# A bidirectional SSD mixer on one core: another order of a group's stages, with the state products placed between the parts of the next projection

## The chip, the cores and the metric

The kernel runs on one core of a Trainium2 chip. The metric is the device time of one execution in microseconds (us). Three runs of the kernel before took 1614.75, 1614.91 and 1621.10 us; their median is 1614.91.

## The reference

A trunk of two layers works on 512 tokens of 1024 features, batch 1, in float32. Layer 0 mixes tokens with a bidirectional Mamba-2 (SSD), layer 1 with a two-sided Hyena convolution; each is followed by a SwiGLU and a gated embedding. The change touches the SSD mixer alone:

```python
z, xbc, dt = split(h @ in_w)                    # 2048, 2048 + 2*8*128, 64 columns
xbc = silu(centred_depthwise_conv(xbc, 5 taps)) # x, B, C
for each direction, chunk of 128 tokens:        # 8 groups of 4 heads of 64
    acum = cumsum(dt * a)
    scores = (C @ B.T) * exp(acum_l - acum_s) * dt      # masked, per head
    y = scores @ x + (C @ state) * exp(acum)
    state = state * exp(acum_last) + B.T @ (exp(acum_last - acum) * dt * x)
y = (y_f + y_b + x * d_skip) * silu(z)
y = y / rms(y over a group's 256 features) * norm_w
out = y @ out_w
```

## The kernel before, in words

**Matmuls.** A float32 weight is split into a rounded part `w_hi` and a rest `w_lo`, an activation likewise, and a product is three matmuls (`mm3`, L291 to L293) per tile of 128x128 weights and 512 tokens. `dense` (L295) runs such products over a list of tiles. Matmuls of full float32 (transposes, state work) show twice in the trace for one in the code where they are not transposes.

**Weights.** All weights lie in DRAM in the order of use, in blocks of 8 tiles. `weight` (L277) emits a block (`emit_block`, L267) up to two blocks ahead: a transfer on SP's queue (L269), the cast to `w_hi` on ScalarE (L273), the difference `w_lo` on VectorE, or on GpSimd for every second block here (L274). There are three buffers each of raw, hi and lo. One group of the mixer takes six blocks: B, C, x0, x1 and two for z.

**The mixer.** `ssd` (L540) goes over 8 groups `g`. For one group:
- `mix_in` (L575) projects 128 features each of B, C, x0, x1. The evacuation is the convolution: one ScalarE operation (L581) and four on VectorE (L585), then tanh and one more operation (L587, L588).
- `mix_z` (L659) projects the gate.
- `mix_pre` (L674) transposes B (L678) and x (L685), forms CB, the product of C and B by chunk (L690), the weighted inputs `xw` (two operations of VectorE, L698), the state sums `contribution` (L709, four matmuls in `pS`) and the `carry` from chunk to chunk: copies on ScalarE (L718, L720), a product on GpSimd into the scratch tile `stt` (L714), a sum on VectorE (L715). The result is `ST`, the states at the chunks' entries. Last it starts `y` as x times `d_skip` on GpSimd (L730).
- `mix_exp` (L734) makes the decay matrices `M` of the four heads: a broadcast transfer into `FB` on SP's queue (L740, 512 KB, four buffers), two selects on GpSimd (L742), eight exponentials on ScalarE (L746), an add and a product on VectorE (L748, L749).
- `mix_rest` (L752) does the products within chunks (L759) and adds them to `y` (L761), then the state products for each of the four chunks (L765), scales them into `yo` (L768) and adds (L770), then gates (L773 to L775) and takes the sums of squares (L778) with a scratch tile that has the same two buffers as `stt`.
- `scales` and `finish` (L781, L787) normalise two groups at a time and transpose them for the output projection (L793, L322, L323).

PSUM has four buffers `mm` for projections and four `aux` for everything else.

**What sets the order.** The loop at L809 is staggered by one group: while group g is projected, group g - 1 is finished. But the program's order is only a priority. The framework in which the kernel is written lays out each engine's queue when the program is built: it keeps a model of the engines' times and gives each engine, whenever that model has it free, the instruction that stands earliest in the program among those that are ready, and it takes buffers in the same way. On the chip each queue then runs in that fixed order and waits where the chip is later than the model. So instructions of later stages are found between those of earlier ones; the time line of TensorE shows C's matmuls of the next group between two state products.

The loop's order before is this, for an iteration g:

```python
mix_in(g: C, x0, x1); mix_exp(g-1); mix_z(g); mix_in(g+1: B)
mix_rest(g-1); finish(g-3) if g is odd; mix_pre(g); finish(g-2) if g is odd
```

Of the kernel before, what the change touches and what calls it, by code (L numbers as in the profile page):

```python
# [35 lines left out]
def order_mk(name, ms, ks, hold=0):  # L36
    """(name, k, m) in the order of use; the first `hold` columns get their last k late."""
# [143 lines left out]
def constants():  # L181
# [7 lines left out]
    # token order: parity, block of 128, place  # L189
# [5 lines left out]
    # [q, p, (par, blk), 256]  # L195
    out["dec"] = np.ascontiguousarray(dec[perm].reshape(4, P, 4, 256).transpose(2, 1, 0, 3))
    # angular frequencies w and pi / 2 - w, for w = 2 pi (f + 1/2) / 1024, f < 128
    fr = (np.concatenate([np.arange(P), 255 - np.arange(P)]) + 0.5) * (2.0 * math.pi / 1024.0)
    n = np.arange(T)
    cs = np.stack([np.cos(np.outer(n, fr)), np.sin(np.outer(n, fr))])  # [cs, n, f]  # L200
    ch = cs[:, perm].reshape(2, 2, 2, P, 256)  # [cs, par, blk, p, f]
    out["CH"] = np.ascontiguousarray(ch.transpose(3, 1, 0, 2, 4).reshape(P, 2048).astype(f))
    perm = np.array([4 * m + r for r in range(4) for m in range(P)])
    cf = cs[:, perm, :P].reshape(2, 4, P, P)  # [cs, r, m, f]
    out["CF"] = np.ascontiguousarray(cf.transpose(2, 1, 0, 3).reshape(P, 1024).astype(f))
    ci = cs.reshape(2, P, 2, 2, 2, P) / 512.0  # [cs, m, b, par, fch, f], t = 4 m + 2 b + par
# [8 lines left out]
def body(ctx, tc, d, out_):  # L215
# [24 lines left out]
    # ---- constants and parameters  # L240
# [13 lines left out]
    # ---- weight stream  # L254
# [40 lines left out]
    def dense(keys, rhs, evac, at=0, then=None):  # L295
        """keys in order of use; rhs[k] = (hi, lo); evac(m, ps); then() after the first `at` keys"""
# [16 lines left out]
    # ---- norms: sum of squares over features, on every partition  # L313
    def split(src, hi=None, lo=None, scale=None):
        """src * scale as hi + lo"""
# [10 lines left out]
    class Norm:  # L326
# [15 lines left out]
        def finish(self, keep=True):  # L342
            """1 / rms per token as a column, then as a row on every partition"""
# [23 lines left out]
    # ---- Hyena filters in the frequency domain  # L367
# [16 lines left out]
    def forward_h(C, mv, U, pool):  # L384
        """As forward and butterfly, for the cosines of one series and the sines of another:
        even and odd places apart; mv(cs, par, blk) = (hi, lo), [128, 256]"""
# [18 lines left out]
    def forward(CF, mv):  # L405
        """Sums over m of 256 channels' places t = 4 m + r times cos (cs 0) and sin (cs 1) of w t, at 128 w:
        [cs, 0] and [cs, 1] with r = 0, 1 and 2, 3 for cos, r = 1, 0 and 3, 2 for sin.
        mv(cs, r) = (hi, lo), [128 m, 256]"""
# [106 lines left out]
    def after(ins, f, *args):  # L515
        if ins is None:
            return f(*args)
        with tc.issue_after(ins.ins):
            return f(*args)

    # ---- per-layer embedding projection
    def ple_in(pool, i, tags):
        pr = {}
        for k in range(2):
# [602 lines left out]
```

## Time and profile before

| | us |
|---|---|
| median of three runs | 1614.91 |
| span of the profiled execution, first to last instruction | 1613.2 |
| its own time beyond the span | not listed; the median is 1.7 more than the span |
| TensorE busy (matmul) | 1569.7 |
| VectorE, ScalarE, GpSimd busy | 1055.6, 675.9, 203.1 |
| mixer loop, z of group 1 to z of group 7 | 96 to 386 |
| granted TensorE clock, mean | 0.996 of full speed |

How to read it: times in views are us from the span's start, durations of single instructions in a table of lines are ns. PE is TensorE's matmuls, PEld its weight loads, DVE VectorE, ACT ScalarE, POOL GpSimd, SP the queue that issues transfers (SPq is its sequencer). `L765` is line 765 of the kernel. `out<-in` are tile names. In brackets, or behind the last bar, stands idle time before an instruction and what ended it. Matmuls overlap each other, so the pace is read from start to start, not from their durations.

### The profile page before, as it was taken

To read this page: it belongs to the slowest core of one execution; us is meant where nothing else is said; L and a number is where in the kernel's file an instruction comes from. 1 tells how busy PE (TensorE), PEld (TensorE's weight loads), DVE (VectorE), ACT (ScalarE), POOL (GpSimd) and SP (SyncE) were. 2 spreads that over 40 slices of the span, in tenths; PEclk is the share of its full clock that TensorE was granted. 3 is DMA by queue.
4 is the path that set the end of the run, shared out by engine and by line. 5 is a ranking of instruction groups with operands and counts; after the bars stand their busy time and mean duration, and the time that the engine had idled before them with its cause. 6 is when DMAs were issued, how large, how long until landed. Compare 5 with 4: busy or idle time off the path is not lost.

```text
span 1613.2 us, 19944 instructions
## 1 busy us (share of the span) xinstructions
PE 1569.7 (97%) x7746; PEld 1303.4 (81%) x7746; DVE 1055.6 (65%) x1447; ACT 675.9 (42%) x1111; POOL 203.1 (13%) x153
## 2 busy tenths in 40 slices
PE   8999999999999999999999999999999999999998
PEld 5888777878788788888888887788888888888887
DVE  6778987879855765464345578999874434434464
ACT  6575555756434332232233445333243223222355
POOL 1244433443100000000000001332000000000000
PEclk9999999999999999999999999999999999999999
DMA  6343324343133233342333345333122332322332
GB/s 241 113 151 109 114 78 122 113 120 116 53 134 118 79 131 118 104 137 92 98 98 94 103 148 172 105 104 100 58 92 92 93 103 92 104 93 93 122 98 79
DMA packets 56006, 176.80 MB, mean 110 GB/s; under 512 B 5959, under 2 KB 7175, under 8 KB 54760
## 3 DMA queue, kind: packets, MB, share of 16 engines
q1 hardware_dynamic: 46864, 151.17, 29.5%
q10 hardware_dynamic: 9048, 24.36, 4.2%
q8 instruction: 61, 1.00, 0.3%
q14 instruction: 33, 0.27, 0.1%
HBM read 164.89 MB, written 10.62 MB: 109 GB/s over the span
## 4 chain that ended last, share of the span: by engine, by line
PE 72%; DVE 16%; DMA 4%; ACT 4%; issue 2%; POOL 1%; SPq 0%; ACTq 0%; DVEq 0%; POOLq 0%
PE mm_ps L291 21%; PE mm_ps L293 21%; PE mm_ps L292 21%; DMA FB<-FRd 3%; DVE pre L585 2%; DVE w_lo L274 2%; DVE xw L698 1%; PE aux_ps L292 1%; PE aux_ps L291 1%; PE aux_ps L293 1%; DVE M L748 1%; ACT w_hi L273 1%; ACT FB L746 1%; DVE act L320 1%; POOL FB L742 1%
## 5 line engine op out<-in xcount | busy, mean ns | idle before, releaser
L291 PE MATMUL mm_ps<-act,w_hi 128*128 128x512 f32 (+1 forms) x1856 | 722.5, 390 | 0.0
L292 PE MATMUL mm_ps<-act,w_hi 128*128 128x512 f32 (+1 forms) x1856 | 720.9, 388 | 0.9 <-DVE act L320 0.9
L293 PE MATMUL mm_ps<-act,w_lo 128*128 128x512 f32 (+1 forms) x1856 | 719.4, 388 | 0.2 <-DVE w_lo L274 0.2
L273 ACT CAST w_hi<-w_raw 128x1024 fp32r<-128x1024 f32 x248 | 259.8, 1051 | 603.9 <-PE mm_ps L292 427.5
L291 PEld LDWEIGHTS mm_ps<-act,w_hi 128*128 128x128 f32 x1856 | 348.6, 188 | 74.7 <-issue 5.5
L292 PEld LDWEIGHTS mm_ps<-act,w_hi 128*128 128x128 f32 x1856 | 348.6, 188 | 73.9 <-issue 3.6
L293 PEld LDWEIGHTS mm_ps<-act,w_lo 128*128 128x128 f32 x1856 | 348.7, 188 | 72.0 <-issue 2.4
L274 DVE TENSOR_TENSOR w_lo<-w_raw,w_hi 128x1024 fp32r<-128x1024 f32 x213 | 265.8, 1249 | 131.9 <-ACT w_hi L273 131.8
L274 POOL TENSOR_TENSOR w_lo<-w_raw,w_hi 128x1024 fp32r<-128x1024 f32 x35 | 97.6, 2790 | 738.1 <-ACT w_hi L273 716.4
L857 DVE TENSOR_TENSOR fb<-mm_ps,R 128x512 f32<-128x512 f32 x44 | 30.4, 692 | 130.7 <-PE mm_ps L293 130.7
L585 DVE SCALAR_TENSOR_TENSOR pre<-mm_ps,par,pre 128x511 f32<-128x511 f32 (+1 forms) x128 | 93.1, 739 | 3.2 <-ACT pre L581 3.0
L746 ACT ACTIVATE FB<-FB,bcol 128x128 f32<-128x128 f32 x256 | 79.8, 392 | 23.0 <-POOL FB L742 22.8
L854 DVE TENSOR_TENSOR fa<-mm_ps,R 128x512 f32<-128x512 f32 x44 | 30.4, 691 | 89.4 <-PE mm_ps L293 89.4
L865 DVE TENSOR_TENSOR h<-h,mm_ps 128x512 f32<-128x512 f32 x48 | 33.0, 687 | 72.8 <-PE mm_ps L293 72.8
L668 PE MATMUL mm_ps<-w_lo,act 128*128 128x256 f32 x256 | 72.6, 284 | 0.0
L669 PE MATMUL mm_ps<-w_hi,act 128*128 128x256 f32 x256 | 72.4, 283 | 0.0
L667 PE MATMUL mm_ps<-w_hi,act 128*128 128x256 f32 x256 | 72.4, 283 | 0.0
L742 POOL TENSOR_SCALAR_AFFINE_SELECT FB<-FB 128x512 f32<-128x512 f32 x64 | 53.6, 861 | 68.1 <-DMA FB<-FRd 60.7
L668 PEld LDWEIGHTS mm_ps<-w_lo,act 128*128 128x128 f32 x256 | 49.1, 192 | 0.3
L667 PEld LDWEIGHTS mm_ps<-w_hi,act 128*128 128x128 f32 x256 | 49.1, 192 | 0.3
L669 PEld LDWEIGHTS mm_ps<-w_hi,act 128*128 128x128 f32 x256 | 49.1, 192 | 0.0
L319 ACT CAST act<-fb 128x512 fp32r<-128x512 f32 x44 | 27.4, 622 | 29.3 <-DVE fb L858 29.3
(261 smaller groups left out, 1633.8 us busy)
## 6 DMA issues: line engine op xcount, KB each, us to landing
w_raw<-W SPq DMA_DIRECT2D x248, 512.0 KB, 3.5
FB<-FRd SPq DMA_DIRECT2D x32, 512.0 KB, 5.4
pjd<-ppo ACTq DMA_DIRECT2D x16, 256.0 KB, 3.6
Hd<-Ht ACTq DMA_DIRECT2D x4, 1024.0 KB, 3.8
Ht<-Hd ACTq DMA_DIRECT2D x4, 1024.0 KB, 4.8
pj<-pjd ACTq DMA_DIRECT2D x12, 256.0 KB, 3.7
h<-xT SPq DMA_DIRECT2D x8, 256.0 KB, 5.7
dec<-dec ACTq DMA_DIRECT2D x4, 512.0 KB, 4.3
```

The costliest lines, as they stand in the source:

```text
L273: A.copy(hi, raw)
L274: (G if pool_lo(b) else V).tensor_sub(lo, raw, hi.bitcast(F32))
L291: PE.matmul(ps, whi, xhi, start=start, stop=False)
L292: PE.matmul(ps, whi, xlo, start=False, stop=False)
L293: PE.matmul(ps, wlo, xhi, start=False, stop=stop)
L585: V.scalar_tensor_tensor(pre[:, a:b], ps[:, a + o:b + o], pc("cw", 5 * c + j), pre[:, a:b], ALU.mult, ALU.add)
L667: PE.matmul(o, xhi[:, cs], whi, start=k == 0 and c % 2 == 0, stop=False)
L668: PE.matmul(o, xhi[:, cs], wlo, start=False, stop=False)
L669: PE.matmul(o, xlo[:, cs], whi, start=False, stop=k == KD - 1 and c % 2 == 1)
L742: G.affine_select(FB[:, dr], FB[:, dr], pattern=[[0, NC], [1 - 2 * dr, P]], compare_op=ALU.is_ge, fill=BIG, base=0, channel_multiplier=2 * ...
L746: A.activation(e, e, AF.Exp, bias=bcol[:, c, dr * 32 + hd:dr * 32 + hd + 1])
L865: V.tensor_add(h[m], h[m], ps)
```

## The change

The stages of a group are cut smaller and put in another order. `mix_pre` becomes `mix_pre_a` (transposes, CB, xw) and `mix_pre_b` (state sums, carries, start of y). `mix_rest` becomes `mix_diag` (products within chunks), `mix_off` (the state product of one chunk) and `mix_gate`. The exponentials of group g - 1 now stand before the projections of group g; the four state products of group g - 1 stand before C, x0, x1 and z; the products within chunks come after z, straight before the transposes; the gate of g - 1 and the first finish come before B of g + 1; and B stands between `mix_pre_a` and `mix_pre_b`. The sums of squares of the pair before are kept in `last`. The instructions themselves, their shapes and buffers are the same. Comments are also removed, without a change of line numbers up to L696.

```diff
-        def mix_pre(g, t):
+        def mix_pre_a(g, t):
...
+            t.update(XT=XT, CB=CB, BT=BT, xw=xw)
+
+        def mix_pre_b(g, t):
+
+            BT, xw = t["BT"], t["xw"]
             pS = {}
...
-            G.tensor_mul(y.rearrange("p c (h x) -> p c h x", h=4), X4, dsk)
-
-            t.update(XT=XT, CB=CB, ST=ST, y=y)
+            G.tensor_mul(y.rearrange("p c (h x) -> p c h x", h=4), t["XT"].rearrange("p c (h x) -> p c h x", h=4), dsk)
+            t.update(ST=ST, y=y)
...
-        def mix_rest(g, t, ssq, slot):
-            Cc, XT, ST, M, y = t["C"], t["XT"], t["ST"], t["M"], t["y"]
+        def mix_diag(g, t):
+
+            XT, M, y = t["XT"], t["M"], t["y"]
...
-            for c in range(NC):
-                a, b = (1, 2) if c == 0 else (0, 1) if c == 3 else (0, 2)
...
+        def mix_off(g, t, c):
+
+            Cc, ST, y = t["C"], t["ST"], t["y"]
+            a, b = (1, 2) if c == 0 else (0, 1) if c == 3 else (0, 2)
+            ps = aux_ps().rearrange("p (a x) -> p a x", a=2)
+            PE.matmul(ps[:, a:b], Cc[:, c * P:c * P + P], ST[:, si(c, a):si(c, b)], start=True, stop=True)
...
+        def mix_gate(g, t, ssq, slot):
+            y = t["y"]
...
             if g < NG:
                 t = ts_[g]
-                if g:
-                    mix_in(g, t, EARLY, 4 * KD)
             if g:
                 mix_exp(g - 1, tp)
+            for i in range(NC):
+                if g:
+                    mix_off(g - 1, tp, i)
+                    if g < NG and i < 3:
+                        mix_in(g, t, EARLY + i * KD, EARLY + i * KD + KD)
             if g < NG:
                 mix_z(g, t)
+            if g:
+                if g % 2:
+                    last, ssq = ssq, pool.tile([P, 2, NC], F32, tag="ssq", name="ssq", bufs=2)
+                mix_diag(g - 1, tp)
+            if g < NG:
+                mix_pre_a(g, t)
+            pair = g > 2 and g % 2
+            if pair:
+                rs = scales(last)
+                finish(g - 3, ys[g - 3], rs)
+            if g:
+                ys[g - 1] = mix_gate(g - 1, tp, ssq, (g - 1) % 2)
             if g + 1 < NG:
                 ts_[g + 1] = {}
                 mix_in(g + 1, ts_[g + 1], 0, EARLY)
-            pair = g > 2 and g % 2
-            if pair:
-                rs = scales(ssq)
-            if g:
-                if g % 2:
-                    ssq = pool.tile([P, 2, NC], F32, tag="ssq", name="ssq", bufs=2)
-                ys[g - 1] = mix_rest(g - 1, tp, ssq, (g - 1) % 2)
-            if pair:
-                finish(g - 3, ys[g - 3], rs)
             if g < NG:
-                mix_pre(g, t)
+                mix_pre_b(g, t)
             if pair:
                 finish(g - 2, ys[g - 2], rs)
```

## Rows read from the trace of the kernel before

**Rows 1.** The page: busy us, share of the span, instructions, by engine.

```profile
PE 1569.7 (97%) x7746; PEld 1303.4 (81%) x7746; DVE 1055.6 (65%) x1447; ACT 675.9 (42%) x1111; POOL 203.1 (13%) x153
```

**Rows 2.** Windows of two groups: length, then busy us of PE, PEld, DVE, ACT, POOL.

```profile
143.56:190.80 47.24, 44.94 (x262) 37.98 (x260) 40.27 (x52) 27.75 (x62) 19.16 (x17) 1.00 0.37 112
...
340.68:386.08 45.40, 44.62 (x261) 38.14 (x260) 33.56 (x46) 25.31 (x56) 18.33 (x17) 1.00 0.40 127
```

**Rows 3.** Waits of PE from 60 to 430: us, times, longest.

```profile
PE aux_ps L709 <- DVE xw L698: 8.9, 8, 1.9
PE aux_ps L765 <- DVE y L761: 6.9, 6, 1.6
PE aux_ps L709 <- ACT w_hi L273: 2.1, 2, 1.1
PE aux_ps L678 <- DVE yo L768: 0.6, 1, 0.6
```

**Rows 4.** Time line of PE in one group: start, us, engine, line, operation.

```profile
155.07 0.40 PE L291 MATMUL mm_ps<-act,w_hi 128*128 128x512 f32 x1
...
160.31 0.39 PE L293 MATMUL mm_ps<-act,w_lo 128*128 128x512 f32 x1
...
165.00 0.79 PE L291 MATMUL mm_ps<-act,w_hi 128*128 128x512 f32 x1
...
167.53 1.12 PE L765 MATMUL aux_ps<-ST,sC 128*128 128x512 f32 x2 [1.51 <-DVE y L761]
...
172.34 1.06 PE L690 MATMUL aux_ps<-sC,sB 128*128 128x128 f32 x8
...
177.94 2.35 PE L709 MATMUL aux_ps<-xw,BT 128*128 128x256 f32 x6
```

**Rows 5.** Time line of DVE around the same group.

```profile
145.65 0.68 DVE L748 TENSOR_TENSOR M<-FB 128x512 f32<-128x512 f32 x1
...
148.17 2.31 DVE L748 TENSOR_TENSOR M<-FB 128x512 f32<-128x512 f32 x1
...
163.75 2.48 DVE L274 TENSOR_TENSOR w_lo<-w_raw,w_hi 128x1024 fp32r<-128x1024 f32 x1 [3.65 <-ACT w_hi L273]
...
173.51 2.45 DVE L698 TENSOR_TENSOR xw<-XT,wS 128x768 f32<-128x768 f32 x1
...
176.82 0.95 DVE L698 TENSOR_TENSOR xw<-XT,wS 128x768 f32<-128x768 f32 x1
...
189.06 0.74 DVE L715 TENSOR_TENSOR ST<-stt,aux_ps 128x256 f32<-128x256 f32 x2
```

**Rows 6.** Time line of PE in group 7, the first L709.

```profile
413.16 0.70 PE L709 MATMUL aux_ps<-xw,BT 128*128 128x256 f32 x2 [0.62 <-DVE xw L698]
```

**Rows 7.** Lines of DVE from 96.2 to 428.5: busy us, mean ns, idle before.

```profile
L768 DVE TENSOR_TENSOR yo<-aux_ps,eF 128x256 f32<-128x256 f32 (+1 forms) x30 | 15.8, 546 | 0.5 <-PE aux_ps L765 0.5
...
L761 DVE TENSOR_TENSOR y<-y,aux_ps 128x512 f32<-128x512 f32 x16 | 10.8, 676 | 0.8 <-PE aux_ps L759 0.8
```

**Rows 8.** Time line of PE in the next group, the last six L709.

```profile
230.19 2.39 PE L709 MATMUL aux_ps<-xw,BT 128*128 128x256 f32 x6 [1.91 <-DVE xw L698]
```

**Rows 9.** Time line of DVE in that group, the last state.

```profile
234.44 0.41 DVE L715 TENSOR_TENSOR ST<-stt,aux_ps 128x256 f32<-128x256 f32 x1
```

**Rows 10.** Time line of ACT in both groups: each time the last square.

```profile
185.34 0.40 ACT L778 ACTIVATE junk<-y 128x256 f32<-128x256 f32 x1
...
228.25 0.40 ACT L778 ACTIVATE junk<-y 128x256 f32<-128x256 f32 x1
```

**Rows 11.** Time line of POOL in the group of rows 4.

```profile
173.25 1.90 POOL L730 TENSOR_TENSOR y<-XT,par 128x1024 f32<-128x1024 f32 x1 [8.10 <-DVE y L770]
...
185.12 1.32 POOL L742 TENSOR_SCALAR_AFFINE_SELECT FB<-FB 128x512 f32<-128x512 f32 x2 [3.37 <-DMA FB<-FRd]
```

**Rows 12.** Waits of DVE from 96 to 430: us, times, longest.

```profile
DVE ST L715 <- POOL stt L714: 6.0, 9, 2.5
```

**Rows 13.** Waits of SP's queue from 60 to 430: us, times, longest.

```profile
SPq L740 <- DVE M L748: 95.6, 25, 15.3
```

More of the change, by code (lines that the diff above doesn't have):

```diff
@@ L761, in mix_rest @@
                 V.tensor_add(y[:, 2 * cp:2 * cp + 2], y[:, 2 * cp:2 * cp + 2], ps)
-            for c in range(NC):
-                a, b = (1, 2) if c == 0 else (0, 1) if c == 3 else (0, 2)
-                ps = aux_ps().rearrange("p (a x) -> p a x", a=2)
-                PE.matmul(ps[:, a:b], Cc[:, c * P:c * P + P], ST[:, si(c, a):si(c, b)], start=True, stop=True)
-                yo = npool.tile([P, 2, 4, 64], F32, tag="sq", name="yo", bufs=2)
-                ef = eF[:, c].rearrange("p (a x) -> p a x", a=2)[:, a:b, 4 * g:4 * g + 4].unsqueeze(3).broadcast_to([P, b - a, 4, 64])
-                V.tensor_mul(yo[:, a:b], ps.rearrange("p a (h x) -> p a h x", h=4)[:, a:b], ef)
-                for i in range(a, b):
-                    V.tensor_add(y[:, c], y[:, c], yo[:, i].rearrange("p h x -> p (h x)"))
+        def mix_off(g, t, c):
[3 more added lines that the diff above has]
+            PE.matmul(ps[:, a:b], Cc[:, c * P:c * P + P], ST[:, si(c, a):si(c, b)], start=True, stop=True)
+            yo = npool.tile([P, 2, 4, 64], F32, tag="sq", name="yo", bufs=2)
+            ef = eF[:, c].rearrange("p (a x) -> p a x", a=2)[:, a:b, 4 * g:4 * g + 4].unsqueeze(3).broadcast_to([P, b - a, 4, 64])
+            V.tensor_mul(yo[:, a:b], ps.rearrange("p a (h x) -> p a h x", h=4)[:, a:b], ef)
+            for i in range(a, b):
+                V.tensor_add(y[:, c], y[:, c], yo[:, i].rearrange("p h x -> p (h x)"))
+        def mix_gate(g, t, ssq, slot):
+            y = t["y"]
             if g == 0:
```

## The prediction

> **What bounds the kernel now.** I read the busy times of the page first. TensorE is busy for 1569.7 of 1613.2 us, every other engine for 65% or less [rows 1]. So a change can gain only by closing gaps between matmuls, and it can lose on any engine whose lateness reaches TensorE.
>
> Next come the windows, one per group of the first mixer [rows 2]. Two groups with the same matmuls, busy 44.9 and 44.6 us on TensorE, last 47.2 and 45.4 us. The difference is waiting, not computing.
>
> The waits of TensorE in this stage name it [rows 3]. Matmuls of L709 (state sums) wait 8.9 us for xw and 2.1 us more behind a late weight cast. Matmuls of L765 (state products) wait 6.9 us for the adds of L761. That is 17.9 us, 1.1% of the kernel, and nearly all that TensorE waits for in the stage.
>
> One group in order of time shows how [rows 4]. The B projection of the next group starts at 155.07 and its 24th matmul at 160.31: with the pace of 0.23 us, 5.47 us in all. The products within chunks (L759) follow, then the state products (L765), with C's matmuls of the next group pulled between them, as the one at 165.00. The pulled matmuls are not enough: L765 stands still 1.51 us until L761 has freed an aux buffer of PSUM. Then come the transposes and L690 (starts at 172.34, ends at 173.40), and in the end L709, the last of which ends at 180.29.
>
> VectorE explains the lateness [rows 5]. It sat 3.65 us waiting for a weight cast and then did w_lo in 2.48 us, so y came late. The first xw took 2.45 us, the second 0.95 us.
>
> **The change part by part.** No instruction is added or removed: every term is a wait that goes or comes.
>
> *B between the transposes and the state sums.* Today the second xw ends at 177.77 [rows 5], 4.4 us after L690 ends at 173.40 [rows 4]. After the change 5.47 us of B stand in this place, work that needs nothing of xw. So the waits of L709 go wherever a B follows, which is in groups 0 to 6. Group 7 has no B; its wait of 0.62 us [rows 6] stays. The term is 8.9 + 2.1 - 0.6 = 10.4 us gained. Bounds: 0 if VectorE is later by as much as it has gained in cover; 10.4 if not. In the groups with two finished outputs xw may end later than in this one, but there the new order also puts xw ahead of the gate, and eight more transposes ahead of B. I take the full term.
>
> *State products spread over C, x0 and x1.* Each of the first three products now has a projection of 5.47 us behind it and the fourth the gate projection, while VectorE's part in one is 0.55 us for L768 [rows 7] and one or two adds of the same width or less. Four products no longer ask for aux buffers in a row right after L759. All 6.9 us go; the bounds are 0 and 6.9, and I take 6.9, since the cover is several times the need.
>
> *Products within chunks straight before the transposes.* Now the transposes ask for aux buffers right behind L759: two of the four are free, two come free with the two adds of L761, 0.68 us each [rows 7]. Bounds per group: 0, and 1.4 us if both adds are waited for in full. Such a wait of a transpose shows once in the stage, 0.6 us [rows 3]; nearer to that than to the full adds in every group I take 0.2 us in 8 groups, 1.6 us lost.
>
> *The first state product now soon after the carries.* This is the new wait that I fear. Before, three projections and the gate projection lay between the last state (L715) and L765. Now the product of chunk 0 needs the last backward carry, and in the program nothing for TensorE but the second finish of a pair stands between; C comes behind it. TensorE can do C's matmuls meanwhile if its queue is laid so, but a product laid at the planned moment waits for whatever is later than planned. How long is the chain on the chip? In the group of [rows 4] L709 ends at 180.29 and the last state at 189.80 [rows 5], 9.5 us. In the next group it is 232.58 to 234.85, 2.3 us [rows 8, 9]. The difference is the gate: the scratch tile of L778 shares its two buffers with the carries' product on GpSimd (L714). In the slow group the last of the four squares ran at 185.34 [rows 10], and GpSimd then still had to finish two selects that had waited 3.37 us for a transfer [rows 11]. In the quick group the last square was done by 228.65 [rows 10], before L709's. The change puts the gate ahead of B, so the quick case becomes the rule, and 2.3 us lie well within C's 5.47. Bounds per group: 0, and 9.5 - 5.5 = 4.0 us. I take 0.67 us, what VectorE waits for GpSimd at this step today (6.0 us in 9 waits [rows 12]), as it is the same step and the same two engines: 7 groups, 4.7 us lost.
>
> *The exponentials ahead of C, x0 and x1.* Per group four broadcast transfers on SP's queue, eight selects on GpSimd, 32 exponentials on ScalarE and eight operations on VectorE move past three projections, and so past three weight transfers and their casts. Such a transfer has waited up to 15.3 us in SP's queue for its buffer [rows 13], with weight transfers behind it. What hides that is the weight stream's run of two blocks ahead, 2 x 5.47 = 10.9 us; today, with the same queueing, no wait for a weight over the 2.1 us already counted is listed in the stage [rows 3]. I cost it at nothing. Bounds: 0, and 15.3 - 10.9 = 4.4 us in a group whose cover is gone. The adds of M that now stand in front of the convolutions on VectorE delay the release of C's PSUM bank. It is next needed at the gate projection, two projections or 10.9 us later: nothing lost.
>
> **Sum.** -10.4 - 6.9 + 1.6 + 4.7 = -11.0 us. The profiled execution's span of 1613.2 becomes 1602.2. Its own total is not listed; the median of the three runs, 1614.9, is 1.7 us over the span, which I keep: 1603.9, say **1604 us**.
>
> **The rivals.** A measurement of this kernel can tell some 0.5%, 8.1 us, from no change.
>
> *Carries late by one slow add (1611 us).* The adds of M read two SBUF tiles. One took 0.68 us and the next 2.31 us [rows 5]; the xw of 2.45 us, the same kind of operation, began while GpSimd was busy with y from 173.25 to 175.15 [rows 11]. The change lets the adds of M start before the convolutions, beside the carries on GpSimd. One such add ahead of the last state makes it 1.63 us late: 7 x 1.63 = 11.4 us in place of 4.7, and -17.3 + 1.6 + 11.4 = -4.3 us. For it: four adds and eight selects per group now crowd into that stretch. Against: the states stand earlier in the program and go first when both are ready.
> The Trainium skill, "SBUF — State Buffer", section Who interferes with whom, says that an operation of VectorE with two SBUF inputs and one of GpSimd that reads SBUF exclude each other, the later one waiting out the whole instruction. The long xw agrees with it, as does the short one after y was done. By that rule a slow add is the normal case, and the sum would be this rival's 1611.
>
> *First product held up by the whole chain (slower, 1627 us).* If a select that waits for its broadcast is still laid ahead of the carries, the 9.5 us chain stays and L765 waits 4.0 us in 7 groups: 28.0 - 17.3 + 1.6 = +12.3 us. It decides from 3.4 us per group on ((17.3 - 1.6 + 8.1) / 7). For it: today a select's wait ended just ahead of the carries [rows 11]. Against: with the gate gone from there, the carries are ready before the broadcast is.
>
> *The order does not come out as written (1615 us).* The queues are laid by readiness, as C's matmul between two L765 shows [rows 4]. If B is pulled forward in the same way, it covers other gaps than the two, and the waits stay as they are.
>
> **How the numbers follow.** Forecast 0.50, slow add 0.24, order as before 0.10, whole chain 0.16. Faster by over 0.5%: nearly all of the forecast and a quarter of the slow-add case, 0.52; slower: the whole-chain case, 0.16; the rest, 0.32, is within. The range goes down to 1597, where both waits go and nothing comes (-17.3), and up to 1618, which takes in the slow add, the unchanged order and a little over, and leaves out the whole chain and the tails. The forecast's own range is 1597 to 1607.
>
> **What would show it.** In the waits of the changed kernel L709 should have under 2 us and L765 none for L761. B's 24 matmuls should stand between L690 and L709, and one L765 within or after each of C, x0, x1. A wait of L765 for L715 and of a transpose for L761 should be the new entries, about 5 and 2 us. I am wrong if L765 waits over 2 us per group for the states, if waits for a weight cast appear, or if L709 still waits with B in front of it.

## The result and the profile after

The changed kernel takes 1634.5 us in the median, the kernel before 1614.8 us: 1.0117 times as long (95% interval 1.0103 to 1.0131). It is slower by 1.2%, outside the range, and nearest to the rival in which the first state product is held up by the whole chain of states.

The lines have moved a little: the state sums are L713 now (L709 before), their copies L722 and L724, the carries L718 on GpSimd and L719 on VectorE, the state product L772 (L765), its scaling L775, the products within chunks L763, their add L765 (L761), the squares L788, the finish L803, the selects L745, the exponentials L749.

The busy times of the page, which answer to [rows 1]:

```profile
PE 1576.5 (97%) x7746; PEld 1310.9 (80%) x7746; DVE 1059.6 (65%) x1447; ACT 676.1 (41%) x1111; POOL 199.1 (12%) x153
```

The same 7746 matmuls are busy for 6.8 us more; the span grew from 1613.2 to 1631.9 us, 18.7 us. The rest is waiting. The waits of TensorE from 60 to 470 us (us in all, times, longest), to be held against [rows 3]:

```profile
PE aux_ps L772 <- DVE ST L719: 12.4, 5, 4.1
PE aux_ps L772 <- DVE rs L794: 9.4, 2, 5.1
PE aux_ps L772 <- ACT sB L587: 4.8, 1, 4.8
PE aux_ps L803 <- ACT ST L722: 2.3, 2, 1.2
PE aux_ps L803 <- DVE act L323: 0.6, 1, 0.6
```

Both old waits are gone: no state sum waits for xw, no state product for the add of y. In their place the first state product of every group waits, 12.4 + 9.4 + 4.8 = 26.6 us in 8 waits. The names rs and sB in the second and third row mislead. The time line shows what ends these waits: in the group below the last carry ends at 187.57 and the product begins at 187.71, while the reciprocal that the row names has nothing to do with the product.

That group in order of time, on four engines (start, us, engine, line, operation; in brackets the idle time before it):

```profile
175.91 2.74 PE L713 MATMUL aux_ps<-xw,BT 128*128 128x256 f32 x8
...
176.51 1.91 POOL L745 TENSOR_SCALAR_AFFINE_SELECT FB<-FB 128x512 f32<-128x512 f32 x2 [4.18 <-DMA FB<-FRd]
177.42 1.57 ACT L749 ACTIVATE FB<-FB,bcol 128x128 f32<-128x128 f32 x5 [2.91 <-POOL FB L745]
...
178.90 0.40 ACT L788 ACTIVATE junk<-y 128x256 f32<-128x256 f32 x1
...
180.50 0.39 ACT L749 ACTIVATE FB<-FB,bcol 128x128 f32<-128x128 f32 x1
180.79 1.04 ACT L273 CAST w_hi<-w_raw 128x1024 fp32r<-128x1024 f32 x1
181.73 0.77 ACT L581 ACTIVATE pre<-mm_ps,par 128x512 f32<-128x512 f32 x1
...
182.40 0.35 ACT L722 COPY ST<-aux_ps 128x256 f32<-128x256 f32 x1
...
182.91 1.28 POOL L718 TENSOR_TENSOR stt<-ST,eL 128x256 f32<-128x256 f32 x2 [1.80 <-ACT ST L722]
...
183.72 0.41 DVE L719 TENSOR_TENSOR ST<-stt,aux_ps 128x256 f32<-128x256 f32 x1
184.04 0.74 DVE L585 SCALAR_TENSOR_TENSOR pre<-mm_ps,par,pre 128x511 f32<-128x511 f32 x1
184.14 1.22 POOL L745 TENSOR_SCALAR_AFFINE_SELECT FB<-FB 128x512 f32<-128x512 f32 x2
...
185.33 0.61 POOL L718 TENSOR_TENSOR stt<-ST,eL 128x256 f32<-128x256 f32 x1
...
187.15 0.42 DVE L719 TENSOR_TENSOR ST<-stt,aux_ps 128x256 f32<-128x256 f32 x1
...
187.71 1.19 PE L772 MATMUL aux_ps<-ST,sC 128*128 128x256 f32 x2 [4.27 <-DVE rs L794]
...
227.90 2.74 PE L713 MATMUL aux_ps<-xw,BT 128*128 128x256 f32 x8
...
231.63 0.37 ACT L724 COPY ST<-aux_ps 128x256 f32<-128x256 f32 x1
...
236.46 0.42 DVE L719 TENSOR_TENSOR ST<-stt,aux_ps 128x256 f32<-128x256 f32 x1
```

The last three rows are of the next group, and are needed further down. In the first, the sums end at 175.91 + 2.74 = 178.65. The first state copy needs nothing but them, yet it starts at 182.40. Ahead of it on ScalarE's queue stand exponentials, which sat 2.91 us idle for a select of GpSimd, then four squares of the gate, one more exponential, a weight cast and a convolution's first step. The copies done, the carries are not quick either: between the adds of VectorE stand the convolution steps of B (L585), between the products of GpSimd the selects. From the last sum to the last state it is 187.57 - 178.65 = 8.9 us. In groups 1, 2, 4 and 6, called single groups from here on, it is 8.5 to 9.8 us; in groups 3 and 5, behind which a pair is finished, 6.2 to 7.0 us; in groups 0 and 7, the ends of the loop, 7.15 and 5.0 us. What stands between the sums and the product on TensorE's queue is 21 matmuls of C in a single group, 21 x 0.23 = 4.8 us; it is 14 in group 0 and 11 in groups 3 and 5.

The wait is paid twice. Windows of the same stretch (length, busy us of PE, PEld, DVE, ACT, POOL, then TensorE's granted clock, DMA share, GB/s):

```profile
183.50:187.70 4.20, 0.00 (x0) 0.02 (x1) 3.89 (x9) 4.16 (x9) 4.20 (x8) 0.74 0.65 214
187.70:192.30 4.60, 4.59 (x9) 2.98 (x10) 2.87 (x8) 4.31 (x12) 1.38 (x2) 0.50 0.00 2
192.30:197.50 5.20, 5.20 (x25) 4.26 (x24) 5.20 (x12) 4.00 (x14) 1.00 (x1) 1.00 0.33 101
```

TensorE stands still for 4.2 us, and then runs 4.6 us at a granted clock of 0.50 (1.2 GHz) before the clock is back at 1.00: 4.6 x 0.50 = 2.3 us more.

The account: waits from 18.9 us (8.9 + 6.9 + 2.1 + 0.6 as in [rows 3] and 0.4 in smaller rows) to 29.5 us, +10.6. Of the other 8.1 of the 18.7 us, 6.8 are the longer busy time of the same matmuls, which I put down to the clock, and 1.3 are smaller waits, most of them outside the stage.

### The profile page after: what moved, and what is told of

Same layout as the page of the kernel before. It is cut to its first block, busy times and chain, and to the rows that moved or that the text cites. A ratio compares the mean times of both kernels' runs of the same rounds, so it can differ in the third digit from the quotient of the medians.

```text
span 1631.9 us, 19935 instructions
## 1 busy us (share of the span) xinstructions
PE 1576.5 (97%) x7746; PEld 1310.9 (80%) x7746; DVE 1059.6 (65%) x1447; ACT 676.1 (41%) x1111; POOL 199.1 (12%) x153
## 4 chain that ended last, share of the span: by engine, by line
PE 66%; DVE 8%; issue 1%; ACT 1%; DMA 0%; POOL 0%; DVEq 0%; ACTq 0%; POOLq 0%
PE mm_ps L291 20%; PE mm_ps L292 20%; PE mm_ps L293 20%; PE aux_ps L291 1%; PE aux_ps L293 1%; PE aux_ps L292 1%; DVE act L320 1%; DVE w_lo L274 1%; DVE act L1023 1%; DVE U L1060 0%; DMA pjd<-ppo 0%; DVE pl L320 0%; PE aux_ps L772 0%; PE aux_ps L497 0%; DVE pq L1069 0%
## 5 line engine op out<-in xcount | busy, mean ns | idle before, releaser
L274 DVE TENSOR_TENSOR w_lo<-w_raw,w_hi 128x1024 fp32r<-128x1024 f32 x213 | 261.7, 1230 | 96.0 <-ACT w_hi L273 95.8
L585 DVE SCALAR_TENSOR_TENSOR pre<-mm_ps,par,pre 128x511 f32<-128x511 f32 (+1 forms) x128 | 94.3, 742 | 6.1 <-ACT pre L581 5.1
L749 ACT ACTIVATE FB<-FB,bcol 128x128 f32<-128x128 f32 x256 | 79.4, 392 | 18.6 <-POOL FB L745 18.5
L772 PE MATMUL aux_ps<-ST,sC 128*128 128x256 f32 (+1 forms) x64 | 31.6, 589 | 26.6 <-DVE ST L719 12.4
L745 POOL TENSOR_SCALAR_AFFINE_SELECT FB<-FB 128x512 f32<-128x512 f32 x64 | 51.5, 825 | 34.8 <-DMA FB<-FRd 31.8
```

Of the source, the lines that this page charges most:

```text
L274: (G if pool_lo(b) else V).tensor_sub(lo, raw, hi.bitcast(F32))
L585: V.scalar_tensor_tensor(pre[:, a:b], ps[:, a + o:b + o], pc("cw", 5 * c + j), pre[:, a:b], ALU.mult, ALU.add)
L745: G.affine_select(FB[:, dr], FB[:, dr], pattern=[[0, NC], [1 - 2 * dr, P]], compare_op=ALU.is_ge, fill=BIG, base=0, channel_multiplier=2 * ...
L749: A.activation(e, e, AF.Exp, bias=bcol[:, c, dr * 32 + hd:dr * 32 + hd + 1])
```

## Experiments

I call the framework's model of the engines' times, by which the queues are laid, the planner. The theory after the result: the product's place on TensorE's queue is some 5 us behind the last sum, and the chain of states takes 6 to 10 us from there; the difference is the wait. The main rival: something lengthened the chain, so it is the chain that must be mended, and the place is right. In the diffs the loop is written in short: B, C, x0, x1 and z are the projections, off(0) to off(3) the state products, exp, diag, gate, pre_a, pre_b and finish the stages; unchanged lines without a sign. Every ratio is to the kernel before, with its 95% interval.

**1. The products later.** Two state products behind x0, two behind x1: 48 matmuls, 10.9 us, cover the chain.

```diff
-off(0); C; off(1); x0; off(2); x1; off(3); z
+C; x0; off(0); off(1); x1; off(2); off(3); z
```

> The changed kernel with one edit: the state products of chunks 0 and 1 stand after x0, those of 2 and 3 after x1. Between the last state sum and the first product 48 projection matmuls (10.9 us) then lie on TensorE's queue in place of 21 (4.8 us). Theory (the product is laid where the planner believes the carries done, and on the chip they are done 9.1 to 9.6 us after the state sums): 10.9 is more than that, the waits of the state products (26.6 us in the profile) go, TensorE's clock stays up, both old waits stay away: 1597 to 1603 us. Rival (the exponentials now ahead of the projections crowd ScalarE and VectorE and the lateness reaches TensorE anywhere): the wait moves on, to the gate projection's banks or to a weight, and the time stays over 1615 us.

1603.1 us, ratio 0.9936 (0.9921 to 0.9951). Waits of TensorE in the stage:

```profile
PE aux_ps L803 <- ACT ST L722: 4.3, 2, 2.1
PE mm_ps L293 <- DVE w_lo L274: 1.5, 1, 1.5
PE aux_ps L772 <- DVE ST L719: 0.5, 1, 0.5
```

Of 26.6 us in L772 0.5 us is left, and the span falls by 30.5 us, to 1601.4. So it is the place of the product that costs the time. The rows that are left are 6.3 us, most of it transposes of the finish that wait for a state copy, and the two gains together reach the end.

**2. B's move alone.** All else in the order of before.

```diff
 C; x0; x1; exp; z
-B; diag; off(0..3); gate; finish; pre_a; pre_b; finish
+diag; off(0..3); gate; finish; pre_a; B; pre_b; finish
```

> One part alone: the order of the kernel before, but B of the next group between the transposes with xw and the state sums. Theory: the waits of the state sums for xw go (10.4 us), the waits of the state products for their aux buffers stay (6.9 us), no new wait, as four projections lie between carries and products: 1603 to 1607 us. Rival (B in that place is what makes the carries late and costs by itself): over 1612 us.

1609.0 us, 0.9971 (0.9960 to 0.9981). A gain of 4.6 us, less than expected:

```profile
PE aux_ps L713 <- ACT junk L788: 5.3, 2, 2.6
PE aux_ps L678 <- DVE yo L775: 2.5, 2, 1.2
PE aux_ps L685 <- DVE yo L775: 1.9, 4, 0.6
PE aux_ps L713 <- DVE xw L697: 1.6, 2, 1.0
```

The waits for xw are down to 1.6 us, but sums wait 5.3 us in two of the pair groups, behind ScalarE, and the transposes 4.4 us for buffers that the state products hold. Taking the products away from there is what the spreading is good for.

**3. The spreading alone**, with B ahead of the products within chunks as before.

```diff
 exp; off(0); C; off(1); x0; off(2); x1; off(3); z
-diag; pre_a; finish; gate; B; pre_b; finish
+B; diag; gate; finish; pre_a; pre_b; finish
```

> The other part alone: the state products spread over the projections, exponentials first, but B straight after z as before. On TensorE's queue the first two products now stand 11 matmuls of C (2.5 us) behind the last state sum. Theory: the states are again later than that by some 3 to 5 us per group and the waits for xw are back: 1630 to 1645 us. Rival (B's evacuation, which the changed order puts ahead of the carries, is the whole cause of the late carries): carries come in time, only the xw waits stay, 1608 to 1613 us.

1622.8 us, 1.0058 (1.0043 to 1.0073), between the two expectations. L772 waits 19.0 us:

```profile
PE aux_ps L772 <- DVE ST L719: 19.0, 8, 3.9
```

Here the product lies only 11 matmuls behind the sums in the single groups and 7 in groups 3 and 5, and the chain behind the last sum is 4.6 to 5.1 us long in groups 1 to 6. Part of that is a head start, as the sums are spread over 3.3 to 4.8 us; from the first sum it is 8.2 to 9.4 us, against 9.0 to 12.5 us in the change. B's evacuation is done before the carries begin in this order, and so are the squares: in group 2 GpSimd's first product sits 4.28 us idle for them. So the spreading loses by itself, and in the change the place of B, with that of the gate, adds to the length of the chain.

**4. The exponentials back to their old rank** in the program, ahead of z.

```diff
-exp; off(0); C; off(1); x0; off(2); x1; off(3); z
+off(0); C; off(1); x0; off(2); x1; off(3); exp; z
```

> The changed kernel with the exponentials put back to where they stood, ahead of the gate projection. Theory (position of the product against the carries): TensorE's queue is the same, the wait stays: 1628 to 1638 us. Rival (the exponentials moved forward hold up the copies and carries): most of the 26.6 us goes, 1600 to 1612 us.

1635.8 us, 1.0148 (1.0127 to 1.0169), as the changed kernel; the chain is 8.2 to 9.8 us in the single groups. The rank changes nothing: in group 2 six exponentials still stand ahead of the state copies. This does not clear the exponentials, as experiment 13 shows.

**5. Product 0 last.** Chunk 0 needs the last carry, chunk 1 an earlier one.

```diff
-off(0); C; off(1); x0; off(2); x1; off(3); z
+off(1); C; off(2); x0; off(3); x1; off(0); z
```

> The changed kernel with the four state products in another order: chunks 1, 2, 3 ahead of C, x0, x1 and chunk 0, whose state is the last of the carries, ahead of the gate projection. Chunk 1 needs two of the four links of the carries less; the planner answers by laying it 11 matmuls (2.5 us) behind the state sums in place of 21 (4.8 us). In the changed kernel's trace the states of chunk 1 are there 6.5 us after the sums in a group without a pair. Theory (what counts is how far the chip is behind the planner, and it is behind from the first copy of a state on): the wait stays at some 4 us per group: 1626 to 1638 us. Rival (the length of the chain counts): two links less are some 2 us per group: 1612 to 1622 us.

1627.3 us, 1.0067 (1.0052 to 1.0082). The planner laid the product earlier in turn, 11 matmuls behind the sums, and L772 waits 20.6 us, 6 us less than in the change. A product that needs less of the chain is laid sooner, and waits all the same.

**6. No broadcast transfers.** My rival had a reason: a select that waits for its broadcast ahead of the carries. Here the 32 transfers are left out, and selects and exponentials work on other numbers, so the decay matrices are not the reference's.

```diff
-nc.sync.dma_start(FB, FRd[:, hd].partition_broadcast(P))
-G.affine_select(FB[:, dr], FB[:, dr], ...)
+G.affine_select(FB[:, dr], h[dr], ...)
```

> The changed kernel without the broadcast transfers of the exponentials: the selects read a tile that is always there, and the exponentials take another bias, so the decay matrices hold other numbers. Leaves out 32 transfers of 512 KB; every other instruction stays. Theory (copies and carries are late because the cast, the evacuation and the convolution of B rank ahead of them on ScalarE and VectorE): the wait of the first state product shrinks by at most a third: 1624 to 1636 us. Rival, and my own forecast's word for the slower case (selects that wait for their broadcast hold up exponentials and copies): over two thirds of the wait goes: 1603 to 1616 us.

1638.7 us, 1.0143 (1.0127 to 1.0159), the chain still 9.5 us in the single groups. Lines are one lower here:

```profile
PE aux_ps L771 <- DVE rs L793: 14.6, 3, 4.9
PE aux_ps L771 <- DVE ST L719: 13.9, 5, 4.8
```

The wait for the transfer, 4.18 us of GpSimd's idle time in the group shown above, is not needed for a chain of this length. But the chain is held up in other places here, and the run does not clear the selects as such. In the same group, whose sums end at 182.16:

```profile
181.16 0.42 ACT L787 ACTIVATE junk<-y 128x256 f32<-128x256 f32 x1 [2.63 <-DVE y L784]
...
183.00 4.68 POOL L744 TENSOR_SCALAR_AFFINE_SELECT FB<-h 128x512 f32<-128x512 f32 x4 [2.95 <-DVE M L750]
...
184.68 0.35 ACT L722 COPY ST<-aux_ps 128x256 f32<-128x256 f32 x1
...
187.65 1.76 POOL L718 TENSOR_TENSOR stt<-ST,eL 128x256 f32<-128x256 f32 x3
```

The copies come behind squares that waited for the gate on VectorE, and the first product of the carries comes behind four selects, 2.35 us after the copies are done. In the changed kernel that product waits for the copy in groups 1, 2, 4, 5 and 6, 7.3 us of GpSimd's idle time in all.

**7. B's evacuation behind the carries** in the program, to clear VectorE between the adds.

```diff
-B; pre_b; finish
+B (matmuls only); pre_b; evacuation of B; finish
```

> The changed kernel with one thing moved: B's matmuls stay between the transposes and the state sums, but B's evacuation (one operation of ScalarE, four of VectorE, tanh and a product) is put behind the carries in the program. The planner then lays the first product 11 matmuls (2.5 us) behind the sums in place of 21 (4.8 us). Theory: without the convolution between them the carries end 5 to 6.5 us after the sums in place of 9.5, the wait is 2.5 to 4 us per group: 1618 to 1630 us. Rival (the convolution does not hold them up): carries stay at 9 us or more, the wait grows to 6 us or more: over 1640 us.

1643.4 us, 1.0170 (1.0152 to 1.0188): slower, a miss. The chain is 1.0 to 1.5 us shorter in the single groups (7.5 to 8.2 us), but the planner laid the product 11 matmuls behind the sums, 2.3 us earlier. The product is L775 in this kernel:

```profile
PE aux_ps L775 <- DVE ST L722: 32.1, 8, 5.8
```

This gain in the chain, which the planner's model also sees, is given back, and more.

**8 to 10. A series of places.** The edit is where the first products stand: behind C (24 matmuls, 5.5 us), in the middle of x0 with the second one behind it (36, 8.2 us), and all behind x1 (72, 16.4 us). The last also has the exponentials behind x1, and the second finish of a pair between the products of the next group.

```diff
-off(0); C; off(1); x0; off(2); x1; off(3); z
+C; off(0); x0; off(1); x1; off(2); off(3); z
```

> The changed kernel with each state product one projection later in the program (chunk 0 after C, 1 after x0, 2 and 3 after x1): 24 projection matmuls, 5.5 us, between the last state sum and the first product in place of 21, 4.8 us. Theory (wait per group = the 9.5 us of the chain in groups without a pair, 6.5 to 7 us in pairs, less the cover, and for each idle stretch near 4 us some 2 us of lowered clock after it): about 0.5 us less wait per group: 1626 to 1633 us. Rival (a place right after the carries in the program, not the cover, was the fault): the wait goes, under 1615 us.

```diff
-off(0); C; off(1); x0; off(2); x1; off(3); z
+C; x0 (first half); off(0); x0 (second half); off(1); x1; off(2); off(3); z
```

> The same, with the product of chunk 0 in the middle of x0: 36 matmuls, 8.2 us, of cover. Theory: 9.5 - 8.2 = 1.3 us of wait in four groups, none in pairs, so some 5 us in place of 30, and the idle stretches are too short in this kernel's traces to lower the clock (in the kernel before, waits of 1.5 us left it at full speed): 1604 to 1610 us. Rival (the clock falls with any wait of the product): 1612 us or more.

```diff
-exp; off(0); C; off(1); x0; off(2); x1; off(3); z
+C; x0; x1; exp; off(0); off(1); finish(g-3, g even); off(2); off(3); z
```

> The other end: all four products after x1, ahead of the gate projection, exponentials behind the projections, second finish of a pair between the products: 72 matmuls, 16.4 us, of cover, 6 us more than the chain needs. Theory: no wait for states is left, as with 10.9 us; four products in a row ask for aux buffers again, but the adds within chunks no longer stand ahead of them: 1598 to 1603 us. Rival (four products in a row wait for their buffers as before the change): 1604 to 1609 us.

| cover of the chain | median us | ratio (95%) | wait of L772 |
|---|---|---|---|
| 4.8 us (the change) | 1634.5 | 1.0117 (1.0103 to 1.0131) | 26.6 us |
| 5.5 us | 1626.1 | 1.0071 (1.0056 to 1.0086) | 19.1 us |
| 8.2 us | 1610.2 | 0.9968 (0.9957 to 0.9979) | 7.0 us |
| 10.9 us (experiment 1) | 1603.1 | 0.9936 (0.9921 to 0.9951) | 0.5 us |
| 16.4 us | 1605.1 | 0.9938 (0.9920 to 0.9955) | 8.2 us |

The cover of the change is that of its single groups. Between the first two rows 6.3 of the 7.5 us of wait go in groups 0, 3 and 5, where the cover rises from 14 and 11 to 24 matmuls. The time falls with the cover until the cover is as long as the chain. Past that nothing is won: in the last row 6.7 of the 8.2 us are products that wait for VectorE's scaling of the one before, since four come close together again; the wait that the spreading took away is back in part:

```profile
PE aux_ps L772 <- DVE yo L775: 6.7, 2, 3.4
PE aux_ps L772 <- DVE ST L719: 1.5, 1, 1.5
```

**11. The gate behind the carries.** Are the squares what the state copies wait for?

```diff
-finish; gate; B; pre_b; finish
+finish; B; pre_b; gate; finish
```

> The changed kernel with one stage moved: the gate of the group before, with its four squares on ScalarE, stands behind the state sums and carries in the program, not ahead of B. The planner leaves the first product where it is in groups without a pair (21 matmuls behind the sums). Theory (the copies of the states are late because the squares, and the exponentials and the cast laid behind them, stand ahead of the copies on ScalarE): copies come 2 us or more earlier, the wait falls to under 2.5 us per group: 1610 to 1622 us. Rival (B's evacuation and the weight cast alone hold the copies): the wait stays near 4 us, 1628 us or more.

1638.7 us, 1.0146 (1.0131 to 1.0162). My theory of that moment fell. The copies still start 2.4 to 3.4 us behind the sums in the single groups (2.4 to 3.75 us in the change): exponentials fill the place that the squares left. In groups 3 and 5 the product waits no more, but there the transposes of the finish wait 7.7 us for a state copy.

**12. Three orders at once.** The exponentials held behind the copies, which alone is experiment 13 below, selects behind the last carry, B's evacuation behind the carries: all that stands in the chain's way, on three engines.

```diff
+after(last carry, G.affine_select ...)
+after(second copy, A.activation ... Exp)
-B; pre_b; finish
+B (matmuls only); pre_b; evacuation of B; finish
```

> The same with two more orders: the selects of a group come behind its last carry on GpSimd, and B's evacuation behind the carries. The product is laid 10 to 12 matmuls (2.3 to 2.7 us) behind the sums. Theory (what stands ahead of the copies and between the links makes up the 9.5 us): carries end 4 to 6 us after the sums, the wait is 1.5 to 3 us, too short for the clock to fall much: 1608 to 1622 us. Rival (the links themselves, with their hand-overs between GpSimd and VectorE, are the chain): carries at 8 us or more, wait over 5 us: over 1635 us.

1612.0 us, 0.9981 (0.9971 to 0.9991). The chain is 3.6 to 4.0 us in the single groups and 2.8 us in groups 3 and 5: a chain near the quick one that I had taken for granted does exist, if it is forced. The product then comes after 10 to 12 matmuls (8 in groups 3 and 5), and still waits 8.9 us in all; the gate's projection waits 6.9 us for a PSUM bank that the convolution (L585), late now, has still to free.

**13. Only the exponentials behind the copies**, by an explicit order on ScalarE's queue; the loop is that of the change.

```diff
-A.copy(ST[:, si(2, 1)], pS[3][:, 0])
+t["cp"] = A.copy(ST[:, si(2, 1)], pS[3][:, 0])
-A.activation(e, e, AF.Exp, bias=...)
+after(t["cp"], lambda: A.activation(e, e, AF.Exp, bias=...))
```

> The changed kernel with one order fixed by hand: on ScalarE the exponentials of a group come behind its two state copies. The planner then lays the first product 15 to 18 matmuls (3.4 to 4.1 us) behind the sums. Theory (exponentials that wait for selects stand ahead of the copies): copies come within 2 us of the last sum in place of 3 to 4.4, the carries end at 7 to 8 us, the wait is 3 to 4 us: 1622 to 1632 us, little gained since the planner moves the product up by as much. Rival (squares, cast and evacuation alone hold the copies): copies stay at 3 us or more, carries at 9.5, wait over 5 us: over 1640 us.

1608.0 us, 0.9962 (0.9947 to 0.9977), better than either expectation. Time line of the same four engines in the same group:

```profile
170.95 2.74 PE L713 MATMUL aux_ps<-xw,BT 128*128 128x256 f32 x8
...
174.07 0.36 ACT L722 COPY ST<-aux_ps 128x256 f32<-128x256 f32 x1
...
174.57 1.76 POOL L718 TENSOR_TENSOR stt<-ST,eL 128x256 f32<-128x256 f32 x3 [6.37 <-ACT ST L722]
...
178.19 0.41 DVE L719 TENSOR_TENSOR ST<-stt,aux_ps 128x256 f32<-128x256 f32 x1
...
178.75 0.67 PE L772 MATMUL aux_ps<-ST,sC 128*128 128x256 f32 x2 [1.62 <-ACT FB L749]
...
184.12 2.10 POOL L745 TENSOR_SCALAR_AFFINE_SELECT FB<-FB 128x512 f32<-128x512 f32 x1 [6.81 <-DMA FB<-FRd]
```

The sums end at 173.69 and the copy starts 0.4 us later, not 3.75 us. The last state ends at 178.60, 4.9 us after the sums (8.9 us in the change). The selects have left too: exponentials that come later free their buffers later, so the next selects run at 184.12, behind all carries. Of the 4.0 us 3.4 lie ahead of the first copy and 0.6 behind it; over the single groups 2.0 to 3.4 us lie ahead and 0.6 to 2.8 us behind, where the selects no longer stand between the carries. The run does not part the exponentials' own time on ScalarE from the wait for selects that they bring with them. Taking the squares away (experiment 11) or the transfers (experiment 6) left the copies late; holding the exponentials behind them does not. So their place ahead of the copies is shown to be the cause of the late copies.

**14, 15. A version that beats both.** Experiment 1 with the second finish of a pair put between the state products of the next group, and the same with the exponentials behind the copies.

```diff
-C; x0; off(0); off(1); x1; off(2); off(3); z
+C; x0; off(0); off(1); finish(g-3, g even); x1; off(2); off(3); z
```

> The version with late state products (the first of the experiments) and the second finish of a pair moved from behind the carries to behind the first two state products of the next group, so that its transposes no longer wait for an aux buffer that a late copy of a state holds. Theory: that wait (4.3 us in two groups) goes: 1597 to 1601 us. Rival (the transposes then wait for something else there): 1602 to 1605 us.

> The fastest version so far (late products, late second finish, 1600.7 us) with the exponentials behind the state copies. Theory: its remaining waits (1.5 us for a state, 2.9 us for a slow addition to y, 1.5 us for a weight) shrink with ScalarE's queue cleared: 1596 to 1600 us. Rival (the exponentials moved out of the idle stretch crowd the projections): 1602 us or more.

1600.7 us, 0.9904 (0.9888 to 0.9919), and 1599.3 us, 0.9904 (0.9889 to 0.9919): both beat the kernel before by 1.0% and the changed one by 2.1%, and the two are not told apart. The waits that are left in the stage in the second one are no longer those of the chain:

```profile
PE mm_ps L291 <- ACT w_hi L273: 3.3, 3, 1.1
...
PE aux_ps L772 <- DVE ST L719: 1.3, 1, 1.3
```

Weight casts come late 3.3 us in all, the first product of one group 1.3 us.

## Why the prediction was wrong

**The two gains were right.** The waits of L709 and L765 [rows 3] went to nothing, even the 0.6 us in group 7 that I had left standing. Experiment 1 shows that the gain reaches the end: with both, and without the new wait, the ratio is 0.9936, or 10.5 us less than the 1613.6 us of the kernel before beside it, against a forecast of 11.0 us. That the two come so close is partly luck: B's move alone brings 4.6 us (experiment 2), and experiment 1 still has waits that the forecast did not count.

**The step that failed is the state product "soon after the carries".** I took 0.67 us in 7 groups, 4.7 us; it was 26.6 us in 8 waits. The step held three readings, and each was off.

The first is the length of the chain. I took the 2.3 us of [rows 8, 9] for a quick case. But the group of [rows 8] had its first two sums at 226.00, and its last six at 230.19, because they waited for xw:

```profile
226.00 0.67 PE L709 MATMUL aux_ps<-xw,BT 128*128 128x256 f32 x2 [1.06 <-ACT w_hi L273]
...
230.90 0.37 ACT L720 COPY ST<-aux_ps 128x256 f32<-128x256 f32 x1 [2.16 <-PE aux_ps L709]
```

The chain had begun with the early sums: from 226.00 to 234.85 it is 8.9 us. In the same group of the changed kernel it is 9.0 us from the first sum (227.90) to the end of the last state (236.88), no slower by this measure. By removing the wait for xw, the change also removed this head start: the eight sums now run together in 2.74 us, and 6.2 us of the chain lie behind them in this group, 8.5 to 9.8 us in single ones. The head start is not all of it, though: from the second state copy to the last state it was 3.95 us before (230.90 to 234.85) and is 5.25 us after (231.63 to 236.88), so 1.3 of the 4.0 us by which 6.2 exceeds 2.3 lie in the links themselves. A span between two events must be taken from the event that starts it, not from the last of a row of events.

The second is the cause. I wrote that with the gate out of the way "the quick case becomes the rule". In the single groups the chain behind the last sum took 9.5 to 11.1 us before and takes 8.5 to 9.8 us after, so the slow case stayed the rule. The gate's squares are now early in the program, but on ScalarE they are still done between the sums and the copies (178.90 in the time line), behind exponentials, and when they are moved away exponentials take the place (experiment 11).

The third is the cover. C's 5.47 us were to lie between. The planner laid the product after 21 matmuls or 4.8 us in single groups, after 11 in groups 3 and 5; experiments 3, 5 and 7 show the same, with 11 matmuls in single groups. I take it that the product is pulled to the moment at which the model has the chain done, but the model's own times stand in no run, so this is argued and not shown. By it, it was not chain against cover alone: the chain on the chip is longer than in the model, and the difference is waited for.

**The exponentials at nothing** held for what I priced, their move past three projections: with the old rank the time is the same (experiment 4), and no wait for a weight is listed after. What I did not name are the state copies on the same ScalarE queue. Holding the exponentials behind them, with the selects that then come later too, is worth some 25 us (the ratio goes from 1.0117 to 0.9962 in experiment 13). Before the change the first copy in the group of [rows 4] ran 0.04 us after its two sums (176.01 to 176.71), with no exponential between:

```profile
176.75 0.38 ACT L718 COPY ST<-aux_ps 128x256 f32<-128x256 f32 x1 [2.17 <-PE aux_ps L709]
```

**The transposes' wait for the adds of L761**, 1.6 us in my sum, did not come. In its place the transposes of the finish wait 2.3 us for a state copy, the same late copies again, and 0.6 us for an evacuation.

**The clock is a term that I did not have at all**: some 6.8 of the 18.7 us. It could be seen in the kernel before, once: in group 5 the longest wait, 1.90 us, was followed by 3.4 us at a granted clock of 0.50, in which the six sums took 4.08 us and not 2.35 us as in [rows 4]:

```profile
327.93 4.08 PE L709 MATMUL aux_ps<-xw,BT 128*128 128x256 f32 x6 [1.90 <-DVE xw L698]
...
328.10:331.50 3.40, 3.40 (x6) 1.66 (x6) 1.98 (x5) 0.37 (x1) 0.77 (x2) 0.50 0.60 217
```

**The rivals.** The whole chain's price was well sized: 4.0 us in 7 groups, 28.0 us, where 26.6 us were measured, and it went past the 3.4 us per group from which it decides (26.6 / 7 = 3.8). It gave 1627 us; the 7.5 us from there to 1634.5 are about what the clock took. Its reason, a select ahead of the carries that waits for its broadcast, is there in part: such a select ends just ahead of the first product in group 3, after a wait of 2.54 us, and others stand between the carries in groups 4, 5 and 6 with waits of 0.5 to 1.8 us, the longest this one:

```profile
337.69 0.64 POOL L745 TENSOR_SCALAR_AFFINE_SELECT FB<-FB 128x512 f32<-128x512 f32 x1 [1.76 <-DMA FB<-FRd]
```

But in five groups the first product waits for the copy, and without the broadcasts the time is no shorter (experiment 6). So the size was right in part by luck. I gave it 0.16 because the gate was to be gone: a price may be right and its chance wrong, if the chance hangs on one supposed cause. The slow add is not what made the carries late: in the group shown no add of M stands between the copies and the last state, only convolution steps. The adds of M from 96 to 430 us, before and after (ns, least, median and longest; first and last start):

```profile
L748 DVE TENSOR_TENSOR M<-FB x29: 675/680/2886, 99.0 to 420.9; 128x512 f32<-128x512 f32 x29
...
L751 DVE TENSOR_TENSOR M<-FB x26: 675/688/1661, 117.6 to 425.1; 128x512 f32<-128x512 f32 x26
```

The mean falls from 1238 to 1006 ns. Every add that begins while GpSimd is idle takes 0.68 us, 15 before and 13 after. Of those that begin while it works, 11 of 14 took 1.1 to 2.9 us before, and 12 of 13 take 1.1 to 1.7 us after. The Trainium skill, "SBUF — State Buffer", section Who interferes with whom, would have these adds slow, with selects and carries on GpSimd at the same time, and the rows agree. What did not follow is the price: the slow adds fall in other places than the last links of the carries. The order came out as written: B stands ahead of the sums, and none of them waits for xw.

## What to carry to other kernels

Where a consumer is brought close behind a chain of small steps over several engines, measure that chain from the event that starts it, and count on the consumer's queue the work that the planner really leaves in between; a step saved that the planner's model also sees can make the consumer come earlier and wait no less (experiment 7). Put a fixed amount of other work between by the program's order, here two projections for a chain of up to 10 us. More is not better by itself: with 16.4 us of cover four products stood close together and waited for one another. Look for work without a due time, as the exponentials here, that fills a queue ahead of a link of the chain.

## What the runs showed of the hardware

The cost of a stall on TensorE is not only its length. After 4.2 us without a matmul the clock was granted at 0.50 for 4.6 us of work, 2.3 us on top. In the changed kernel this came after six of the eight waits of the product, 2.4 to 5.1 us long, and not after the two of 1.6 and 0.5 us. Length alone does not decide it: in the kernel before a stall of 1.90 us in group 5 was followed by 3.4 us at 0.50, while stalls of 1.91 us [rows 8] and 1.51 us [rows 4] left the clock at 1.00. The Trainium skill, "TensorE: Matmul & The Clock Gate", section What's actually happening, calls the half rate the default state, from which activity frees the engine, and these rows agree.
